# First projections fed from two weight streams, with their conversions ranked ahead of the normalisation

## The chip, the cores and the metric

The kernel runs on one core of one Trainium2 chip. The metric is device microseconds (us) for one execution, the median of several runs. Before the change it is 1677.1 us (three runs, 1676.74 to 1680.07).

## What is computed

One layer of a hybrid trunk on 512 tokens of width 1024, all in float32. Its first steps are what the change touches:

```
h  = rmsnorm(x, norm_mix)                  # x: 512 x 1024
u  = h @ w_in                              # 1024 x 15,616 columns; RWKV, HGRN2, Mamba-2 and gate columns
xw, xa, xg, dt                             # 64 + 64 + 160 + 32 "tail" columns of u
log_w = -exp(-softplus(-(w0 + tanh(xw) @ w_up)) - 0.5)
a     = sigmoid(a0 + xa @ a_up)
y_a, y_b, y_c = rwkv7(u), hgrn2(u), mamba2(u)
merged = gate0*(y_a @ wb0) + gate1*(y_b @ wb1) + gate2*(y_c @ wb2)
x = x + merged @ w_out;  h = rmsnorm(x, norm_ffn)
x = x + (silu(h @ wg) * (h @ wu)) @ w_ffn_out;  out = rmsnorm(x, norm_final)
```

## The kernel before

Every dense product is done in three TensorE passes: activations and weights are each split into a high part (rounded to fp32r) and a low part (the rest), and high times high, high times low and low times high are added in one PSUM bank. The normalised activations are kept transposed as `hh` and `hl`, [128 x 8 x 512].

Weights come in granules of 512 values per partition. `wcols` (L596) makes one: one or two DMAs into a raw tile, a copy on ScalarE (ACT) into the high tile, a subtraction on VectorE (DVE) into the low tile. A stream is a set of places: stream `w` has two raw places (`wr`) and four high and low ones (`wh`, `wl`), L1629; stream `rg` has two of each (`rgr`, `rgh`, `rgl`), L1406. A third raw tile of a stream can be loaded only when the first has been converted and subtracted.

`front` (L683) loads x in four tiles, normalises them and transposes them through PSUM into `hh` and `hl`, first for tokens 0 to 255, then for 256 to 511 (`norm_half`, L648). `tails` (L712) then makes the first projections: 128 columns into bank `d` (two granules) and 64 columns into bank `g` (one granule of 8 x 64, loaded by two DMAs of 8 x 32 columns), both by `dense_halves` (L663), which does each half of the tokens separately, and 128 columns into bank `rw` (two granules) by `dense_h`. From `d`, `g` and `rw` come the inputs of the RWKV decay and gate. `r_stage1` (L794) is the first step of a pair of RWKV heads and takes its weights from stream `rg`; the other mixers and the gates fill TensorE between the steps of the eight pairs.

What order each engine runs is not the order of the code. All operations are recorded with a rank `prio`, and `flush` (L302) lists them: at each step the engine that is free first takes, of its operations that are ready by the planner's own costs, the one with the lowest rank, and among equals the one recorded first. `front` is recorded at rank 0, `tails` and the first `r_stage1` at rank 1, HGRN2 at 2, Mamba-2 at 3, the gates at 4, the merge at 5, the tail of the layer at 6. A granule's DMAs, copy and subtraction take at most rank `WP` = 1. On the chip each engine runs its list strictly as written; SyncE (SP) issues all DMAs from one list.

Of the kernel before, what the change touches and what calls it, by code (L numbers as in the profile page):

```python
# [20 lines left out]
P = 128  # L21
# [5 lines left out]
OFF_TAIL = 3 * RW  # L27
# [4 lines left out]
OFF_DT = OFF_XBC + 3072  # L32
# [42 lines left out]
class Queue:  # L75


    def __init__(self, rec, name):
        self.rec, self.name = rec, name
# [330 lines left out]

class Kern:
    WP = 1

    def __init__(self, tc, ctx, A, consts, out):
        self.tc, self.nc, self.ctx, self.A, self.out = tc, Recorder(tc), ctx, A, out
# [180 lines left out]
    def wcols(self, W, r0, kk, pieces, st="w"):  # L596


        nc = self.nc
        pool, size, bufs, rsize, rbufs = self.wst[st]  # L600
        n = kk * sum(w for _, w in pieces)
        raw = self.t(pool, [P, rsize], st + "r", bufs=rbufs)
        wh = self.t(pool, [P, size], st + "h", dt=F32R, bufs=bufs)
        wl = self.t(pool, [P, size], st + "l", dt=F32R, bufs=bufs)
        v = lambda x: x[:, 0:n].rearrange("p (k c) -> p k c", k=kk)
        prio, nc.prio = nc.prio, min(nc.prio, self.WP)
        c = 0
        for c0, w in pieces:
            nc.sync.dma_start(out=v(raw)[:, :, c:c + w],
                              in_=W[r0:r0 + kk * P, c0:c0 + w].rearrange("(k p) c -> p k c", p=P))  # L610
            c += w
        nc.scalar.copy(out=wh[:, 0:n], in_=raw[:, 0:n])
        self.nlo += 1
        eng = nc.vector if self.lo_dve and self.nlo % self.lo_dve == 0 else nc.gpsimd
        eng.tensor_tensor(out=wl[:, 0:n], in0=raw[:, 0:n], in1=wh[:, 0:n].bitcast(F32), op=ALU.subtract)
        nc.prio = prio
        return v(wh), v(wl)
# [94 lines left out]
    def tails(self, rk):  # L712

        nc, A, cp = self.nc, self.A, self.mx
        W = A["w_in"][0]
        r = lambda tag: self.t(cp, [P, S], tag, dt=F32R)
        lain, sg0, sg1 = (self.t(rk, [P, S], g) for g in ("Ei", "kk", "k"))
        ps2, ps, ps3 = self.psg(), self.psd(), self.psr()
        self.dense_halves([(ps, W, [(OFF_TAIL, P)]), (ps2[0:64], W, [(OFF_TAIL + 256, 32), (OFF_DT, 32)])], lambda: "w")
        self.load_consts(rk)  # L720
        self.load_params0(rk)
        self.dense_h(ps3, [(OFF_TAIL + P, P)], "w")
        self.mix(lain, ps, self.pc("mu", 24), self.omu[:, 24:25])
        H = (slice(0, 64), slice(64, 128))
        nc.scalar.activation(lain[H[0]], lain[H[0]], AF.Tanh)

        self.lora = [r("xw"), r("xa")]
        for i, x in enumerate(self.lora):
            nc.scalar.copy(out=x[H[i]], in_=lain[H[i]])
            nc.vector.tensor_tensor(out=x[H[1 - i]], in0=lain[H[i]], in1=x[H[i]].bitcast(F32), op=ALU.subtract)  # L730
        self.mix(sg1[0:32], ps2[0:32], self.mu1[:, 0:1], self.mu1[:, 1:2])
        nc.scalar.activation(sg1[0:32], sg1[0:32], AF.Sigmoid)
        self.mix(sg0, ps3, self.pc("mu", 25), self.omu[:, 25:26])
        nc.scalar.activation(sg0, sg0, AF.Sigmoid)
        self.sg0 = (r("sg0h"), r("sg0l"))
        self.split(*self.sg0, sg0)

        self.sg1 = r("sg1")
        for b in (0, 32):
            nc.scalar.copy(out=self.sg1[b:b + 32], in_=sg1[0:32])  # L740
        nc.vector.tensor_tensor(out=self.sg1[64:96], in0=sg1[0:32], in1=self.sg1[0:32].bitcast(F32), op=ALU.subtract)

        self.dto = self.t(rk, [P, 4, P], "Ot")
        for c in range(NT):
            nc.vector.tensor_copy(out=self.dto[c * 32:c * 32 + 32, 0], in_=ps2[32:64, c * P:(c + 1) * P])
# [913 lines left out]
```

## Time and profile before

| | |
|---|---|
| median of three runs | 1677.1 us |
| the profiled execution | 1676.58 us, span 1674.8 us |
| TensorE (PE) busy | 1620.5 us, 97% |
| VectorE (DVE) busy | 1023.8 us, 61% |
| ScalarE (ACT) busy | 849.3 us, 51% |
| DMA | 192.08 MB, 115 GB/s over the span |
| chain that ended last | PE 71%, DVE 5%, ACT 4%, DMA 4% |

The span runs from the first to the last instruction of the profiled execution; 1.8 us of its time lie around it. A row of a timeline gives the start, the duration, the engine, the line, the operation and its tiles; the bracket says how long the engine had been idle before and what ended that. Matmuls of one run overlap in the records, so their cost is the distance between their starts.

### The profile page before, as it was taken

Reading aid. Unit: us, or ns where it says so; the run is one execution under the profiler, and the core shown is the slowest. Engines: PE = TensorE matmul, PEld = TensorE weight load, DVE = VectorE, ACT = ScalarE, POOL = GpSimd, SP = SyncE. Lnnn points to the kernel's source line nnn. Section 1 sums busy time; section 2 is a strip of 40 time slices with the busy share of each in tenths; the row PEclk is TensorE's granted clock in tenths of the full one; section 3 lists DMA queues with packets and bytes.
Section 4 is the critical chain, followed back from the end, with each engine's and each line's share of the span. In section 5 each row is a group of like instructions: output and inputs, shape, how many; then the busy total and the mean of one; then the engine's idle time right before and its main releaser. Section 6 shows DMA issues by size and latency. Waiting matters only on the chain.

```text
span 1674.8 us, 31996 instructions
## 1 busy us (share of the span) xinstructions
PE 1620.5 (97%) x12302; PEld 1317.1 (79%) x12302; DVE 1023.8 (61%) x2327; ACT 849.3 (51%) x1533; POOL 262.8 (16%) x285
## 2 busy tenths in 40 slices
PE   6999999999998999999999999999999999999998
PEld 5787787778777877787897787777888888888886
DVE  5787978878887879557558646344354433333233
ACT  6656655655565556567468745324334433333222
POOL 1123231322132222012033112011020000000000
PEclk9999999999999999999999999999999999999999
DMA  5333324333233334334434545877472333333232
GB/s 166 81 90 87 85 69 101 90 96 79 69 86 84 85 78 112 91 98 114 111 107 143 166 124 187 256 213 227 151 223 74 110 94 95 94 94 94 97 95 76
DMA packets 291320, 192.08 MB, mean 115 GB/s; under 512 B 59053, under 2 KB 255047, under 8 KB 291167
## 3 DMA queue, kind: packets, MB, share of 16 engines
q1 hardware_dynamic: 291167, 190.04, 39.8%
q8 instruction: 96, 1.57, 0.4%
q14 instruction: 57, 0.47, 0.1%
HBM read 164.22 MB, written 25.76 MB: 113 GB/s over the span
## 4 chain that ended last, share of the span: by engine, by line
PE 71%; DVE 5%; ACT 4%; DMA 4%; issue 2%; SPq 0%; POOL 0%; POOLq 0%; ACTq 0%; DVEq 0%
PE d L402 20%; PE rd L402 13%; PE g L402 9%; PE m L402 8%; PE rw L402 7%; PE rs L402 7%; PE ru L402 7%; ACT L399 1%; DMA ydram<-y 1%; DMA em<-ydram 1%; DVE cb L402 1%; DMA ab<-ydram 1%; DVE X L402 1%; DMA gwr<-in_w_in_dram 1%; DMA cb<-dcum 0%
## 5 line engine op out<-in xcount | busy, mean ns | idle before, releaser
L402 DVE TENSOR_TENSOR wl<-wr,wh 128x512 fp32r<-128x512 f32 x267 | 187.4, 703 | 260.7 <-ACT wh L402 256.9
L402 ACT CAST wh<-wr 128x512 fp32r<-128x512 f32 x267 | 164.8, 619 | 321.4 <-PE d L402 97.4
L402 ACT CAST rgh<-rgr 128x512 fp32r<-128x512 f32 x142 | 87.8, 618 | 192.7 <-PE rd L402 96.3
L402 DVE TENSOR_TENSOR rgl<-rgr,rgh 128x512 fp32r<-128x512 f32 x142 | 102.0, 719 | 107.0 <-ACT rgh L402 105.0
L402 PE MATMUL d<-hh,wh 128*128 128x512 f32 (+1 forms) x368 | 148.2, 403 | 4.7 <-ACT sg L402 2.5
L399 ACT ACT_TABLE_LOAD x115 | 147.5, 1283 | 2.0
L402 PE MATMUL d<-hh,wl 128*128 128x512 f32 (+1 forms) x368 | 145.8, 396 | 1.1 <-DVE wl L402 1.1
L402 PE MATMUL d<-hl,wh 128*128 128x512 f32 (+1 forms) x368 | 145.4, 395 | 0.0
L402 PE MATMUL rd<-hh,rgh 128*128 128x512 f32 (+1 forms) x324 | 130.1, 402 | 2.8 <-DVE k L402 1.6
L402 PE MATMUL rd<-hh,rgl 128*128 128x512 f32 (+1 forms) x324 | 128.2, 396 | 0.0
L402 PE MATMUL rd<-hl,rgh 128*128 128x512 f32 (+1 forms) x324 | 128.0, 395 | 0.0
L402 PEld LDWEIGHTS d<-hh,wh 128*128 128x128 f32 x368 | 70.1, 190 | 22.4 <-ACT sg L402 3.3
L402 PE MATMUL g<-hh,gwh 128*128 128x512 f32 x192 | 79.3, 413 | 7.8 <-ACT gwr L402 4.4
L402 PEld LDWEIGHTS d<-hh,wl 128*128 128x128 f32 x368 | 70.0, 190 | 16.2 <-DVE wl L402 1.4
L402 PEld LDWEIGHTS d<-hl,wh 128*128 128x128 f32 x368 | 69.9, 190 | 13.4 <-issue 1.0
L402 PE MATMUL g<-hh,gwl 128*128 128x512 f32 x192 | 78.4, 409 | 0.2
L402 PE MATMUL g<-hl,gwh 128*128 128x512 f32 x192 | 76.7, 400 | 0.0
L402 PE MATMUL d<-wh,hh 128*128 128x256 f32 x256 | 74.3, 290 | 2.0 <-DVE q L402 0.9
L402 PEld LDWEIGHTS rd<-hh,rgh 128*128 128x128 f32 x324 | 60.9, 188 | 19.3 <-DVE k L402 2.7
L402 PE MATMUL d<-wl,hh 128*128 128x256 f32 x256 | 73.2, 286 | 0.0
L402 PE MATMUL d<-wh,hl 128*128 128x256 f32 x256 | 72.6, 284 | 0.0
L402 PEld LDWEIGHTS rd<-hh,rgl 128*128 128x128 f32 x324 | 60.9, 188 | 14.2 <-issue 0.5
(1514 smaller groups left out, 4235.8 us busy)
## 6 DMA issues: line engine op xcount, KB each, us to landing
wr<-in_w_in_dram SPq DMA_DIRECT2D x108, 256.0 KB
rgr<-in_w_in_dram SPq DMA_DIRECT2D x88, 256.0 KB
wr<-in_w_branch_dram SPq DMA_DIRECT2D x59, 256.0 KB
wr<-in_w_ffn_in_dram SPq DMA_DIRECT2D x58, 256.0 KB
gwr<-in_w_in_dram SPq DMA_DIRECT2D x96, 128.0 KB
rgr<-in_w_ffn_in_dram SPq DMA_DIRECT2D x30, 256.0 KB
wr<-in_w_ffn_out_dram SPq DMA_DIRECT2D x30, 256.0 KB
gdram<-gwr SPq DMA_DIRECT2D x24, 256.0 KB
```

The costliest lines, as they stand in the source:

```text
L399: self.nc.scalar.preload_act_table_set(ops[-1 - j][7])
L402: getattr(getattr(self.nc, eng), method)(*[self.resolve(x) for x in args], **{k: self.resolve(x) for k, x in kw.items()})
```

## The change

The five granules of the first projections no longer all come from stream `w`: an iterator gives them `w`, `rg`, `w`, `rg`, `w`. So the first granule of `d` is `wr`, the second `rgr`, the 64-column granule of `g` is `wr`, the two of `rw` are `rgr` and `wr`. Then, for the three granules of `dense_halves` alone, copy and subtraction get rank -1 (`WC`), ahead of the normalisation's 0; their DMAs keep rank 1. For all later granules `WC` equals `WP` and nothing changes in rank.

```diff
 class Kern:
     WP = 1
+    WC = 1
...
             c += w
+        nc.prio = min(prio, self.WC)
         nc.scalar.copy(out=wh[:, 0:n], in_=raw[:, 0:n])
...
         lain, sg0, sg1 = (self.t(rk, [P, S], g) for g in ("Ei", "kk", "k"))
+
+        early = iter(("w", "rg", "w", "rg", "w")).__next__
+        self.WC = -1
         ps2, ps, ps3 = self.psg(), self.psd(), self.psr()
-        self.dense_halves([(ps, W, [(OFF_TAIL, P)]), (ps2[0:64], W, [(OFF_TAIL + 256, 32), (OFF_DT, 32)])], lambda: "w")
+        self.dense_halves([(ps, W, [(OFF_TAIL, P)]), (ps2[0:64], W, [(OFF_TAIL + 256, 32), (OFF_DT, 32)])], early)
+        self.WC = self.WP
         self.load_consts(rk)
         self.load_params0(rk)
-        self.dense_h(ps3, [(OFF_TAIL + P, P)], "w")
+        self.dense_h(ps3, [(OFF_TAIL + P, P)], early)
```

Because the list is made anew, the order of the whole mixer part moves. PE has 7369 rows of order before and 7426 after (equal instructions in sequence are one row; the instructions are as many). Leaving out the buffer numbers, the orders of PE read alike from row 5184 of before on, which is in the last gate matmuls; the merge, the output projection and the feed-forward part keep their order. ACT loads its tables 116 times before and 112 times after.

In the order before, this is SP's list in the stretch where the 64-column granule is loaded (`wr_232`, by its two DMAs 128x8x32) and then the first granule of `rw` (`wr_295`); `Bt` and `v` are parameters of later steps.

```order
L402 DMA wr_232<-in_w_in_dram 128x8x32
L402 DMA Bt_211<-in_rwkv_gn_b_dram 8x128
L402 DMA Bt_211<-in_hgrn_gn_w_dram 8x128
L402 DMA Bt_211<-in_hgrn_lb_logits_dram 8x128
L402 DMA Bt_211<-in_norm_ffn_dram 8x128
L402 DMA Bt_211<-in_ssm_conv_b_dram 24x128
L402 DMA Bt_211<-in_ssm_gn_w_dram 16x128
L402 DMA v_282<-in_ssm_conv_w_dram 24x512
L402 DMA wr_232<-in_w_in_dram 128x8x32
L402 DMA wr_295<-in_w_in_dram 128x4x128
```

SP's list after the change, from the first weight DMA; the 64-column granule is `wr_108`, those of `rw` are `rgr_159` and `wr_190`, and `E`, `mu`, `a` and `cst` are small parameters and constants.

```order
L402 DMA wr_101<-in_w_in_dram 128x4x128
L402 DMA rgr_103<-in_w_in_dram 128x4x128
L402 DMA wr_108<-in_w_in_dram 128x8x32
L402 DMA cst_110<-in_shape_constants_dram 128x384
...
L402 DMA E_118<-in_rwkv_r_k_dram 8x128
L402 DMA mu_49_150<-in_rwkv_mu_dram 32x1
L402 DMA rgr_159<-in_w_in_dram 128x4x128
L402 DMA a_166<-in_rwkv_w_up_dram 64x128 x2
L402 DMA a_166<-in_rwkv_a_up_dram 64x128 x2
L402 DMA wr_190<-in_w_in_dram 128x4x128
L402 DMA wr_108<-in_w_in_dram 128x8x32
L402 DMA rgr_200<-in_w_in_dram 128x4x128
```

The 64-column granule's first DMA stood in row 28 of SP and is now in row 9; its second stood in row 36 and is now in row 23, behind all four `a` DMAs and `wr_190`, before the `Bt` rows.

ACT's list before, from its last activations of `front` to the read of bank `d` (`Ei`); `rgh` and `gwh` are copies of granules for the first RWKV pair and the first gate.

```order
L402 ACTIVATE hh_168<-m_209,par_135 128x256
L402 CAST rgh_268<-rgr_179 128x512
L402 ACTIVATE hh_168<-rs_236,par_135 128x256
L402 CAST rgh_278<-rgr_183 128x512
L402 CAST gwh_285<-gwr_194 128x256
L402 CAST gwh_289<-gwr_201 128x256
L402 CAST wh_345<-wr_295 128x512
L402 CAST wh_353<-wr_232 128x512
L402 ACTIVATE Ei_362<-d_218,omu_298 128x512
```

ACT's list after, from the last of the four squares of `front`; each `hh` row is an activation of `front`.

```order
L402 ACTIVATE BKt_154,nss_106<-KAo_99 128x1024
L402 CAST wh_170<-wr_101 128x512
L402 CAST rgh_177<-rgr_103 128x512
L402 ACTIVATE hh_182<-m_126,par_136 128x256
...
L402 ACTIVATE hh_182<-rs_131,par_136 128x256
L402 CAST rgh_227<-rgr_159 128x512
L402 ACTIVATE hh_182<-ru_134,par_136 128x256
L402 ACTIVATE hh_182<-m_222,par_136 128x256
L402 CAST wh_250<-wr_190 128x512
L402 ACTIVATE hh_182<-rd_174,par_136 128x256
L402 CAST wh_264<-wr_108 128x512
L402 ACTIVATE hh_182<-m_222,par_136 128x256
```

All five copies now stand among or ahead of the sixteen activations that write `hh`; before, two stood among them and three behind.

PE's list before, at the end of bank `d`'s second half and the start of `rw` and `g`.

```order
L402 MATMUL d_218<-hh_168,wh_203 128x256
L402 MATMUL d_218<-hl_176,wh_203 128x256
L402 MATMUL d_218<-hh_168,wl_276 128x256
L402 MATMUL rw_359<-hh_168,wh_345 128x512
L402 MATMUL rw_359<-hl_176,wh_345 128x512
L402 MATMUL g_366<-hh_168,wh_353 64x256
L402 MATMUL g_366<-hl_176,wh_353 64x256
L402 MATMUL rw_359<-hh_168,wl_356 128x512
```

PE's list after: the end of `d`'s first half, then the borders to `d`'s second half and to `rw`.

```order
L402 MATMUL d_188<-hl_198,rgh_177 128x256
L402 MATMUL d_188<-hh_182,rgl_185 128x256
L402 MATMUL g_290<-hh_182,wh_264 64x256
L402 MATMUL g_290<-hl_198,wh_264 64x256
...
L402 MATMUL g_290<-hh_182,wl_278 64x256
L402 MATMUL d_188<-hh_182,wh_170 128x256
L402 MATMUL d_188<-hl_198,wh_170 128x256
...
L402 MATMUL g_290<-hh_182,wl_278 64x256
L402 MATMUL m_421<-ident_93,E_118 128x66
L402 MATMUL rw_423<-hh_182,rgh_227 128x512
```

Before, `d`'s 48 matmuls came in one piece and those of `g` and `rw` after them; now 24 of `g` stand between the two halves of `d`, 24 behind, and `rw` last.

## Rows read from the trace of the kernel before

**Rows 1.** Busy time by stretch: start:end, length, engines' busy us, PEclk, DMA share, GB/s.
```profile
23.50:26.67 3.17, 0.00 (x1) 0.00 (x1) 0.02 (x1) 0.67 (x2) 0.00 (x0) 1.00 0.85 205
26.67:39.54 12.87, 12.87 (x72) 11.52 (x73) 8.18 (x15) 8.94 (x14) 0.45 (x1) 0.87 0.48 132
39.54:100.00 60.46, 60.46 (x395) 48.39 (x394) 49.36 (x122) 42.54 (x74) 15.49 (x15) 1.00 0.31 80
100.00:1200.00 1100.00, 1066.27 (x9657) 864.77 (x9656) 765.52 (x1864) 623.51 (x1131) 227.76 (x238) 1.00 0.42 119
```

**Rows 2.** PE's timeline, from `d`'s waits to the first HGRN2 matmul.
```profile
19.21 0.39 PE L402 MATMUL d<-hh,wl 128*128 128x256 f32 x1 [0.69 <-DVE wl L402]
19.43 0.28 PE L402 MATMUL d<-hh,wh 128*128 128x256 f32 x1
...
23.21 0.28 PE L402 MATMUL d<-hh,wl 128*128 128x256 f32 x1
26.67 0.50 PE L402 MATMUL rw<-hh,wh 128*128 128x512 f32 x1 [3.17 <-ACT wh L402]
...
35.12 0.40 PE L402 MATMUL rw<-hh,wl 128*128 128x512 f32 x1
...
39.54 0.39 PE L402 MATMUL rs<-xw,lwh 128*128 128x512 f32 x1
...
40.53 0.29 PE L402 MATMUL m<-ident,Bt 82*128 82x82 f32 x1
...
41.34 0.50 PE L402 MATMUL d<-hh,wh 128*128 128x512 f32 x1
```

**Rows 3.** ACT's timeline: activations into `hh`, copies of weights, the long wait.
```profile
10.42 0.82 ACT L402 ACTIVATE hh<-m,par 128x256 fp32r<-128x256 f32 x2
...
12.56 1.17 ACT L402 CAST wh<-wr 128x512 fp32r<-128x512 f32 x2
...
26.00 1.14 ACT L402 CAST wh<-wr 128x512 fp32r<-128x512 f32 x2 [5.49 <-DMA wr<-in_w_in_dram]
```

**Rows 4.** SP's timeline: start and length of DMA issues.
```profile
10.25 0.27 SPq L402 DMA_DIRECT2D E<-in_rwkv_k_a_dram  x1
11.03 0.27 SPq L402 DMA_DIRECT2D E<-in_rwkv_r_k_dram  x1
11.52 0.32 SPq L402 DMA_DIRECT2D mu<-in_rwkv_mu_dram  x1
...
13.13 1.24 SPq L402 DMA_DIRECT2D a<-in_rwkv_a_up_dram  x2
...
19.07 0.38 SPq L402 DMA_DIRECT2D wr<-in_w_in_dram  x1
...
22.17 1.01 SPq L402 DMA_DIRECT2D wr<-in_w_in_dram  x2
```

**Rows 5.** What SP waited for from 7.9 to 12 us: total, times, longest.
```profile
SPq L402 <- DMA wr<-in_w_in_dram: 1.1, 2, 0.6
```

**Rows 6.** Busy time in half microseconds: 256 KB granules (17.0), then the 128 KB of 8x32 columns.
```profile
17.00:17.50 0.50, 0.00 (x0) 0.00 (x0) 0.50 (x2) 0.50 (x3) 0.00 (x0) 1.00 1.15 346
20.00:20.50 0.50, 0.50 (x7) 0.50 (x5) 0.44 (x3) 0.50 (x2) 0.00 (x0) 1.00 0.61 98
20.50:21.00 0.50, 0.50 (x7) 0.50 (x6) 0.50 (x1) 0.01 (x1) 0.00 (x0) 1.00 1.11 176
```

**Rows 7.** DVE's timeline: parts of `hl`, subtractions of weights.
```profile
10.91 0.87 DVE L402 SCALAR_TENSOR_TENSOR hl<-m,par,hh 128x256 fp32r<-128x256 f32 x2
...
13.93 0.68 DVE L402 TENSOR_TENSOR wl<-wr,wh 128x512 fp32r<-128x512 f32 x1
```

**Rows 8.** The page's group of table loads on ACT: busy us, mean ns, idle before.
```profile
L399 ACT ACT_TABLE_LOAD x115 | 147.5, 1283 | 2.0
```

**Rows 9.** A stop of PE among the mixers, in PE's timeline.
```profile
126.95 0.65 PE L402 MATMUL d<-hh,wh 128*128 128x512 f32 x1 [2.19 <-ACT sg L402]
```

**Rows 10.** Busy time in the five microseconds around that stop.
```profile
125.00:130.00 5.00, 3.05 (x8) 2.36 (x9) 3.31 (x10) 4.80 (x6) 0.59 (x1) 0.71 0.60 144
```

## The prediction made before the run

> **What bounds the kernel now.** I read the page's busy shares first: PE is busy for 97% of the span, so the time is PE's work plus PE's idle time plus what a lower clock costs, and since the change neither adds nor removes a matmul, only the last two can move. Then I read busy time by stretch, to find where PE is idle. From 39.54 to 100 us it is not idle at all; from 100 to 1200 us it is idle for 33.7 us of 1100, in many small pieces [rows 1]. The longest piece of the whole run after the first instructions lies at 23.50 to 26.67 us, in the stretch that the diff touches. PE's timeline says who ends it: PE stops 3.17 us for ACT's copy of a weight granule, after 0.69 us for a subtraction a little earlier [rows 2]. ACT's timeline says why the copy is late: ACT itself waits 5.49 us for the DMA [rows 3]. And SP's timeline says why the DMA is late: the 64-column granule (`wr_232`) goes out at 19.07 and, with its second half and the first granule of `rw`, at 22.17 [rows 4]; both raw places of stream `w` were in use until the first two granules were subtracted, and then SP stood behind its parameter rows. So the head of the kernel is bound by two raw places and a list of DMAs.
>
> There is a second cost of that stop. PE's clock is at its full 2.4 GHz while PE is stopped, and in the next stretch, 26.67 to 39.54, the mean granted clock is 0.87 [rows 1]: PE worked for a while at 1.2 GHz. The work there is 48 matmuls of `g` at 0.118 us (33 starts from 19.43 to 23.21 are that far apart) and 24 of `rw` at 0.233 us (19 starts from 35.12 to the next instruction at 39.54) [rows 2]: 5.7 + 5.6 = 11.3 us. It took 12.87, so the low clock cost about 1.6 us.
>
> **The change, part by part.** When is the 64-column granule usable now? Its raw place is free from the start, so its first half goes out early. SP's later waits date the early loads: the three issues at 10.25, 11.03 and 11.52 [rows 4] came when the two weight granules and the constants had landed (SP's waits there are for `wr`, twice [rows 5]). The first half of the new granule is now ahead of the constants in the same list, 128 KB in rows of 128 bytes. The same load took 0.61 + 1.11 shares of half a microsecond, 0.86 us of all DMA engines, where a 256 KB granule moves at 346 GB/s, 0.38 us for as many bytes [rows 6]. So `mu` moves from 11.52 to 12.4, `rgr_159` goes out at 12.75, four `a` issues follow at about 0.62 us each (two took 1.24 [rows 4]) until 15.8, then `wr_190`, then the granule's second half at 16.3. These two are the pair that went out at 22.17 before, in the other order, and were used at 26.00 [rows 3, 4]: 3.8 us. The granule is usable at 15.8 + 3.8 = 19.6 instead of 26.0.
>
> The Trainium skill speaks against that small-row load (DMA: Bandwidth & Descriptors, "Specifications": full rate needs at least 512 bytes; below, the engine reads, modifies and writes). The trace agrees: at the rate of the large granule each half would land 0.5 us earlier, and the sum below would be 1 us better; the measured 0.86 us is what I use.
>
> Copy and subtraction: ACT takes 0.6 us for the copy (two in 1.17 [rows 3]), DVE 0.7 for the subtraction [rows 7]. `g` can start at 20.3 and runs freely from 21.0.
>
> What is paid for it: two copies (1.17 us) now stand ahead of the first `hh` on ACT, and two subtractions (1.3 us) ahead of most of `hl` on DVE; two further copies that wait for DMAs stand among the `hh` rows, so what is behind them on ACT (the last `hh` rows, later `rgh` and `gwh` copies) waits too. DVE then needs nine parts of `hl` at 0.44 (two in 0.87 [rows 7]) after about 13.1, so the first half of `d` cannot end before 17.1; with `rgh_227` waiting for `rgr_159` until 16 to 17 it ends at 17.5 to 18.8. All that is hidden: PE waits for `g`'s granule until 20.3 anyway. Were the granule there at 17, this chain would decide, and the rank -1 would cost what it now hides, some 1.5 us. The second half's `hh` and `hl` rows (six parts, 2.6 us, after 21.0) are due only when `g`'s first 24 matmuls are done, and k by k after that.
>
> PE from there: 22 matmuls of `g` to 23.6, 24 of `d` to 26.4, 24 of `g` to 29.3, a transpose of 0.25, 24 of `rw` at 0.233 to 35.1. Before, `rw` ended at 39.54. Gain: 4.4 us. What is late next is the input of the decay product `rs`. From the end of `g` ACT has to read two banks, load a table (1.28 us [rows 8]), apply two functions and make two copies at about 0.6 us each, and DVE makes two subtractions: 29.3 + 1.3 + 6 x 0.6 + 1.4 = 35.6, or about 36.3 if the copy of an HGRN2 granule that stands ahead of it waits for its DMA. PE has 0.8 us of parameter transposes ahead of `rs` now (40.53 to 41.34 before [rows 2]), so it needs the input at 35.9. I take 0.4 us for this, bounds 0 and 1. Gain 4.0.
>
> The clock: PE stands idle from about 18 to 20.3 and briefly to 21.0, shorter than the 3.17 us that was followed by the low clock, longer than the 0.69 that was not. Bounds: nothing, or a stretch like that of before, 1.6 us. The Trainium skill (TensorE: Matmul & The Clock Gate, "HAM oscillation") has it that a long enough wait for a load throttles PE, so that the next work starts at half rate. If this stop is long enough by that rule, the gain is 2.4 and not 4.0; the trace shows it after one of its two stops at the head. I take the middle, 0.8. Gain 3.2.
>
> The mixers: the planner packs 100 to 1200 us anew. No matmul is added, PE is full from 39.54 to 100 before, so nothing there swallows a shift as long as ACT (42.5 of 60.5 us) and DVE (49.4) keep up [rows 1]. What can change is which stops occur among the mixers. One such stop: PE waits 2.19 us for ACT to read bank `d` [rows 9], because that read stands behind a copy and a table load; and in these 5 us PE is idle for 1.95 us and the clock is 0.71, 1.45 us more [rows 10]. 3.4 us for one stop, either way, and of 33.7 us of idle time there may be several more or fewer. The order gives no sign for one direction (four table loads less on ACT, some more changes of bank on PE), so I take nothing, and keep two such stops, 6.8 us, as both ends.
>
> Sum: 3.2 us off the profiled execution's 1676.58 gives 1673.4. That execution lies 0.5 us under the median of the three runs, so against the median of 1677.1 it is 3.7 us, 0.22%. Differences under 0.2%, 3.4 us, count as no change.
>
> **The rivals.** (1) Slower: the new packing of the mixers meets more stops of PE behind ACT's reads of the banks `d` and `g`, with the low clock behind them. Place: between 100 and 1200 us. Price 3.4 us each; one more cancels the gain, two make it 1680.2, three 1683.6. For it: each bank of these streams exists once, and the table loads stand in front of their reads. Against it: nothing in the change aims there. (2) The same packing meets one stop less and PE's clock holds at the head: 1676.6 - 4.0 - 3.4 = 1669.2. (3) The gain at the head is given back: the copies for the first RWKV pair, made ahead before, now come just in time (their stream carries two of the early granules), and PE stops for them between 36 and 100 us. For it: DVE is busy for 49.4 of 60.5 us there. Against: PE reaches the second of them only some 5 us after `rs`, long after its DMA. 1676.6. (4) The change doesn't do what it says, because the granule's second half, behind the `a` rows on SP, lands late after all. Since `d`'s second half now stands behind `g` on PE, each us of lateness costs one; from 24.7 instead of 20.3 on there is no gain, and if it came at 26.0 as before, the time would be 2 us worse than before, 1678.6.
>
> **How the numbers follow.** Forecast (1670 to 1676): 46%, of it 28 below the bound of 0.2% and 18 within. Rival 1: 16%, slower. Rival 2: 17%, faster. Rival 3: 16%, 14 within and 2 slower. Rival 4: 5%, 3 within and 2 slower. Together faster 45%, within 35%, slower 20%. The likeliest case's own range is 1670 to 1676; the range for 8 in 10 reaches to one stop less at one end and two more at the other, 1667 to 1681.
>
> **What would show it.** In the changed profile: SP issues the second 8x32 load near 16.3; ACT copies the 64-column granule near 19.6; PE's longest stop after its first instruction is about 2.5 us and ends near 20.3 at `g`; no 3 us stop near 24; `rw` ends near 35 (36.8 with the low clock); `rs` follows without a stop over 1 us; PE is full to 100 us. It is wrong if the copy of the 64-column granule begins after 23, if `rs` still starts near 39, or if PE's idle time between 100 and 1200 us differs from 33.7 by more than 4 us: then the packing decides, and not the head.

## The result, and the profile after

The changed kernel takes 1685.1 us, the median of five runs (1682.68 to 1690.36), against 1677.31 us before in the same session (five runs, 1676.74 to 1680.07): a ratio of 1.0051, 95% interval 1.0032 to 1.0069. It is slower, outside the predicted range. Its profiled execution took 1684.33 us, its span is 1682.3 us. Of 7.5 us more span PE is busy for 4.2 (1624.7 after 1620.5, with the same 12,302 matmuls) and idle for 3.3.

The head first. SP's timeline of the changed kernel, with the issue that answers to the last of [rows 4]:

```profile
15.82 1.06 SPq L402 DMA_DIRECT2D wr<-in_w_in_dram  x2
```

The row holds two issues: the second granule of `rw` at 15.82 and the 64-column granule's second half behind it, at 16.37 in the trace (predicted were 15.8 and 16.3). Their counterparts of before went out from 22.17 on. ACT's timeline, as [rows 3]:

```profile
19.99 0.61 ACT L402 CAST wh<-wr 128x512 fp32r<-128x512 f32 x1
...
27.23 0.62 ACT L402 CAST wh<-wr 128x512 fp32r<-128x512 f32 x1 [3.66 <-DMA wr<-in_w_in_dram]
29.85 0.62 ACT L402 CAST wh<-wr 128x512 fp32r<-128x512 f32 x1 [2.00 <-PE m L402]
30.37 0.62 ACT L402 CAST rgh<-rgr 128x512 fp32r<-128x512 f32 x1
31.98 0.62 ACT L402 CAST wh<-wr 128x512 fp32r<-128x512 f32 x1 [0.98 <-DMA wr<-in_w_in_dram]
32.50 0.68 ACT L402 ACTIVATE k<-g,mu 32x512 f32<-32x512 f32 x1
...
36.24 0.62 ACT L402 CAST xw<-Ei 64x512 fp32r<-64x512 f32 x1
```

The granule's copy begins at 19.99 (19.6 predicted). Four copies for later granules stand ahead of the reads of the banks (`k`, `Ei`), three of them behind the end of `g` on PE (29.6). The first of these three waits for PE, the last for its DMA until 31.98; the copy `xw` runs only from 36.24 to 36.86. PE's timeline, as [rows 2]:

```profile
20.65 0.33 PE L402 MATMUL g<-hh,wh 128*64 128x256 f32 x1 [1.97 <-ACT wh L402]
...
21.38 0.33 PE L402 MATMUL g<-hh,wl 128*64 128x256 f32 x1 [0.28 <-DVE wl L402]
...
35.07 0.39 PE L402 MATMUL rw<-hh,wl 128*128 128x512 f32 x1
...
37.72 0.47 PE L402 MATMUL rs<-xw,lwh 128*128 128x512 f32 x1 [1.60 <-DVE xw L402]
```

`g` starts at 20.65 (20.3 predicted), and `rw`'s last matmul gives way to the next row at 35.30 (35.1 predicted, 39.54 before). Up to there everything is where the prediction put it. Then PE stops 1.60 us for the input of `rs`, which DVE finishes with a subtraction behind ACT's copy.

Busy time by stretch shows the rest; the columns are those of [rows 1].

```profile
35.30:39.54 4.24, 2.64 (x12) 1.50 (x10) 3.05 (x7) 4.11 (x8) 0.00 (x0) 1.00 0.05 16
39.54:100.00 60.46, 56.90 (x323) 44.32 (x324) 47.94 (x125) 41.26 (x68) 12.65 (x13) 0.94 0.31 79
100.00:1200.00 1100.00, 1064.93 (x9684) 865.94 (x9684) 764.77 (x1857) 615.91 (x1129) 241.03 (x240) 0.99 0.43 117
```

From 39.54 to 100, where PE was never idle, it is now idle for 3.6 us at a clock of 0.94. From 100 to 1200 it is idle for 35.1 us, only 1.4 more than before, yet the clock reads 0.99 in place of 1.00. So the idle time in the mixers hardly changed, and the clock did. These are the five-microsecond windows of the changed kernel, after 40 us, with a granted clock under 0.8:

```profile
40.00:45.00 5.00, 5.00 (x16) 3.96 (x17) 3.92 (x16) 4.94 (x9) 0.00 (x0) 0.68 0.10 23
90.00:95.00 5.00, 4.88 (x14) 3.88 (x15) 3.90 (x18) 4.34 (x6) 1.65 (x3) 0.66 0.02 5
320.00:325.00 5.00, 5.00 (x17) 3.66 (x15) 4.16 (x14) 3.27 (x5) 1.16 (x1) 0.69 0.41 129
370.00:375.00 5.00, 3.87 (x14) 2.26 (x16) 3.53 (x8) 2.79 (x7) 0.00 (x0) 0.59 0.40 125
375.00:380.00 5.00, 5.00 (x122) 4.56 (x122) 1.81 (x5) 1.19 (x3) 0.00 (x0) 0.73 0.13 36
455.00:460.00 5.00, 3.37 (x70) 3.37 (x74) 1.86 (x4) 1.41 (x4) 0.00 (x0) 0.66 0.10 15
915.00:920.00 5.00, 4.12 (x20) 3.78 (x21) 3.76 (x7) 3.14 (x7) 0.25 (x1) 0.70 0.15 56
920.00:925.00 5.00, 5.00 (x21) 4.28 (x22) 2.96 (x7) 1.50 (x5) 1.17 (x2) 0.62 0.56 184
```

The sum of (1 - clock) x 5 us over all windows from 40 to 1660 us, called *lost clock* below, is 13.5 us. It is 3.45 in the kernel before: the window of [rows 10] and the next, and one more at 515. Two of the eight windows, with 3.3 of the 13.5 us, lie ahead of 100 us; between 100 and 1200 us lost clock is 10.2 us, 6.8 more than before. Lost clock is the most that the low clock can have cost, since matmuls that wait for something else lose nothing. Each stretch has a stop of PE ahead of it. PE's timeline of the changed kernel around one of them, a stop as in [rows 9]:

```profile
90.12 0.50 PE L402 MATMUL rd<-hh,rgh 128*128 128x512 f32 x1 [2.44 <-ACT a L402]
90.46 0.39 PE L402 MATMUL rd<-hl,rgh 128*128 128x512 f32 x1
90.69 0.40 PE L402 MATMUL rd<-hh,rgl 128*128 128x512 f32 x1
90.92 0.57 PE L402 MATMUL rd<-hh,rgh 128*128 128x512 f32 x1
91.29 0.63 PE L402 MATMUL rd<-hl,rgh 128*128 128x512 f32 x1
...
93.85 0.63 PE L402 MATMUL rd<-hl,rgh 128*128 128x512 f32 x1
94.28 0.46 PE L402 MATMUL rd<-hh,rgl 128*128 128x512 f32 x1
94.57 0.39 PE L402 MATMUL rd<-hh,rgh 128*128 128x512 f32 x1
```

After 2.44 us without work the first matmuls start 0.23 us apart, those from 91.29 to 94.28 0.43 apart, then again 0.23: about 3.3 us at 1.2 GHz, some 1.5 us lost. Why PE stopped is told by ACT's timeline of the same kernel:

```profile
86.34 1.15 ACT L402 ACTIVATE X<-X 128x512 f32<-128x512 f32 x2 [0.25 <-DVE X L402]
87.51 1.28 ACT L399 ACT_TABLE_LOAD   x1
88.80 0.69 ACT L402 ACTIVATE tmpA<-rs,par 128x512 f32<-128x512 f32 x1
89.39 0.68 ACT L402 ACTIVATE a<-rd,par 128x512 f32<-128x512 f32 x1
```

Two exponentials of another mixer and a table load stand ahead of `tmpA` and `a`, which reads the bank that PE wants to write.

### The profile page after: what moved, and what is told of

Its sections match the earlier page's. It is cut to its first block, busy times and chain, and to the rows that moved or that the text cites. A ratio compares the mean times of both kernels' runs of the same rounds, so it can differ in the third digit from the quotient of the medians.

```text
span 1682.3 us, 31975 instructions
## 1 busy us (share of the span) xinstructions
PE 1624.7 (97%) x12302; PEld 1321.0 (79%) x12302; DVE 1023.7 (61%) x2327; ACT 843.1 (50%) x1529; POOL 273.0 (16%) x285
## 4 chain that ended last, share of the span: by engine, by line
PE 77%; DMA 8%; DVE 6%; ACT 5%; issue 2%; SPq 1%; POOL 0%; POOLq 0%; ACTq 0%; DVEq 0%
PE d L402 21%; PE rd L402 16%; PE g L402 9%; PE rw L402 8%; PE rs L402 8%; PE ru L402 8%; PE m L402 7%; DMA wr<-in_w_in_dram 2%; ACT L399 1%; DVE X L402 1%; DMA gwr<-in_w_in_dram 1%; SPq L402 1%; DMA ab<-ydram 1%; DMA em<-ydram 1%; DVE wl L402 1%
## 5 line engine op out<-in xcount | busy, mean ns | idle before, releaser
L402 PEld LDWEIGHTS rd<-hh,rgh 128*128 128x128 f32 x324 | 61.5, 190 | 19.6 <-ACT a L402 3.8
```

Of the source, the lines that this page charges most:

```text
L402: getattr(getattr(self.nc, eng), method)(*[self.resolve(x) for x in args], **{k: self.resolve(x) for k, x in kw.items()})
```

## The experiments

Two theories at first: the new packing of the mixers costs the time (P), or the first RWKV pair does, since its stream now also carries early granules (S). The first four kernels take the change apart by its two edits, then by place. All experiments were timed beside the kernel before, but in other sessions than the change, so the ratios are what to compare; all differences are under 1%.

**The streams alone** (copy and subtraction keep their rank):

```diff
-        self.WC = -1
+        self.WC = self.WP
```

> One part alone: the five early granules alternate between the streams, but their copies keep rank 1. Theory P (the loss lies in the new packing of the mixers): the packing is made anew here too, in a third way, so the time is not tied to that of the change: anywhere from 1673 to 1690 us, with the difference to before explained by PE's stops and low clock between 100 and 1200 us. Theory S (the loss comes from the rg stream, which now carries two early granules, so that the first RWKV pair and with it the chain of eight pairs start late): as slow as the change, 1683 to 1687 us.

Measured: 1678.1 us, ratio 1.0012 (1.0000 to 1.0025). S misses; P's range is so wide that it says little here.

**The rank alone:**

```diff
-        early = iter(("w", "rg", "w", "rg", "w")).__next__
+        early = iter(("w", "w", "w", "w", "w")).__next__
```

> The other part alone: all five early granules stay in stream w, and three of them are copied and subtracted ahead of the normalisation. Theory P: a fourth packing, 1673 to 1690 us. Theory S: the rg stream is as before, so the time is that of before, 1677 us, give or take 2.

Measured: 1674.88 us, ratio 0.9997 (0.9984 to 1.0009). The time is that of before, which is S's forecast, but the premise of P did not hold: this is hardly a new packing, since PE has the same instruction at the same place as before in 12,200 of 12,302 matmuls. For the streams alone it is 4839. So the new packing comes with the second stream, and this kernel shows what the earlier conversions are worth without it: nothing that can be measured, though its PE is idle for 4.6 us less up to 39.5 us.

**The new head with the mixers of before**, and **the head of before with the new mixers**: the planner's list is replaced by a stored one, made of the two kernels' lists (the last line of the diff puts that in words).

```diff
-        while left > len(order):
-            ...
+        order = head of one list + what is left, in the other's order
```

> The kernel with the change, but its operations are issued in a stored order: up to the end of bank g's matmuls the order of the change, and from there on every engine takes what is left in the order of before. Theory P: PE's stops and clock among the mixers are those of before, the head keeps most of its 4 us, so 1672 to 1677 us and mean clock near 0.996. Theory S: the early granules still use the rg places, so it is as slow as the change, 1683 to 1687 us.

> The reverse: the kernel before, issued up to the end of bank rw's matmuls in the order of before, and from there on in the order that the change gave to the mixers. Theory P: 1684 to 1690 us with a mean clock near 0.990, like the change. Theory S: the head and the streams are those of before, so 1677 us, give or take 2.

Measured: 1679.02 us, ratio 1.0017 (1.0003 to 1.0031), and 1683.51 us, ratio 1.0050 (1.0032 to 1.0068). The head and the streams of before with the new order of the mixers have the whole loss (0.5 us under P's range); the new head and streams have little of it. S falls. P holds in this, but its 1672 to 1677 for the new head was missed. The stops of over 1 us that PE's timeline of that kernel has between 33 and 46 us:

```profile
36.83 0.47 PE L577 MATMUL rs<-xw,lwh 128*128 128x512 f32 x1 [1.48 <-DVE xw L577]
41.85 0.50 PE L577 MATMUL rd<-hh,rgh 128*128 128x512 f32 x1 [1.96 <-ACT a L577]
```

Both wait for ACT's chain behind the banks: first for `xw`, and 5 us later for `a`. They take most of the head's gain back.

**Three stops to be taken out of the change** by moving ACT's instructions in a stored list (its rows in short):

```diff
-CAST wh (29.85)   -CAST wh (31.98)   ... CAST xa
+CAST xa   +CAST wh   +CAST wh
-ACTIVATE X x2   ACTIVATE tmpA   ACTIVATE a
+ACTIVATE tmpA   ACTIVATE a   ACTIVATE X x2
-CAST wh (455.38)   COPY UV   COPY UV
+COPY UV   COPY UV   CAST wh
```

> The changed program with three local moves in ScalarE's order and nothing else moved: the two copies into `rwh` that stand at 29.85 and 31.98 us go behind the copy of `xa` (they hold the input of `rs` back, PE's stop of 1.60 us at 37.72); `tmpA` and `a` of the second pair (88.80 and 89.39) go ahead of the two exponentials of `X` and their table load (PE's stop of 2.44 us at 90.12); the copy of wh that waited 6.72 us for its DMA at 455.38 goes behind the copies of `UV` (PE's stops of 4.0 us in 450 to 455). Theory P1 (the loss is the sum of single stops of PE, each with its stretch of half clock behind it): the stops give back 1.6 + 2.4 + 4.0 and the low clock behind them 1.6 + 1.7 + 1.7, at most 13.0 us, of which something comes back at other stops: 1673 to 1679, mean granted clock near 0.996. Theory P2 (the packing as a whole sets the length, and a stop that is taken away comes back at the next wait): 1682 to 1687, clock 0.989 to 0.991.

Measured: 1684.28 us, ratio 1.0045 (1.0028 to 1.0062): P2's numbers. But P1 was not tested cleanly, since two of the three stops stayed (1.51 us at `rs`, 1.93 at `a`) and only the third went. Why the first stayed is in DVE's timeline of this kernel:

```profile
35.55 1.29 DVE L576 TENSOR_TENSOR wl<-wr,wh 128x512 fp32r<-128x512 f32 x2 [2.37 <-ACT wh L576]
36.87 0.69 DVE L576 TENSOR_TENSOR xw<-Ei,xw 64x512 fp32r<-64x512 f32 x1
```

ACT's copy of `xw` ended at 34.23, 2.6 us earlier than in the change. DVE's list was left as it was, though: it first takes the subtractions of the two copies that were moved back, and gets to `xw` at 36.87, when it did in the change. At the second stop one of the two exponentials and the table load still ran ahead of `tmpA` (ACT's rows from 87.88). Four windows of this kernel are worth reading all the same:

```profile
40.00:45.00 5.00, 5.00 (x22) 4.04 (x23) 3.91 (x16) 4.94 (x8) 0.00 (x0) 1.00 0.10 24
90.00:95.00 5.00, 3.86 (x10) 3.04 (x11) 1.94 (x9) 4.92 (x7) 0.00 (x0) 0.66 0.23 57
70.00:75.00 5.00, 5.00 (x32) 3.34 (x30) 2.86 (x7) 2.04 (x4) 1.28 (x1) 0.61 0.42 111
455.00:460.00 5.00, 4.35 (x150) 3.85 (x146) 2.28 (x6) 2.24 (x6) 0.00 (x0) 1.00 0.51 125
```

The stop of 1.51 us ahead of 40 us is followed by the full clock here, and by 0.68 in the change; at 455 the low clock went with its stop; at 70 there is a new one, behind a stop of 1.12 us. In these traces the low clock comes behind stops; whether it comes differs from one stop to the next. And it differs between runs of one program: the twelve runs of this kernel go from 1677.01 us at a mean clock of 0.992 to 1692.14 at 0.984, with a correlation of -0.96.

**The first layer's tails ahead of all else in the new head** (ACT's rows in short):

```diff
-ACT: CAST wh, CAST rgh, CAST wh, read g, read d, ... CAST xw, CAST xa
+ACT: read d, CAST xa, ... CAST xw, CAST wh, read g, CAST rgh, CAST wh
```

> The changed head with the operations of the first layer's tails in an order of their own (ScalarE reads `Ei`, `xa` and `xw` right behind the d matmuls, ahead of the copies for the later weights; the 64-column granule's second half and the next granule are asked for ahead of the four loads of `a`), and the order of the kernel before for everything behind. Theory P: the head's gain of 3 to 4 us stays, the mixers go as before: 1671 to 1675. Rival (the head's gain is lost again in the first mixer pair whatever the order, since that pair waits for DMA and not for the head): 1676 to 1680, with stops of PE between 36 and 60 us.

Measured: 1677.94 us, ratio 1.0010 (0.9996 to 1.0025). These are the rival's numbers and place, but not its reason: `rs` starts at 35.57 after a stop of 1.53 us, and at 42.06 PE has stopped 2.71 us for ACT's `a`, not for a DMA; the clock in 40:45 is 0.50.

**Two repackings that have nothing to do with the change.** The planner's costs decide the order; two of them are altered a little in the kernel before.

```diff
-                t += 1.28
+                t += 1.31
```

> The kernel before, with one number of the planner's costs changed (a table load counted as 1.31 in place of 1.28). The work, its pools and the streams are those of before; up to the first four hundred matmuls PE's order is the same, behind them PE has the same instruction at the same place in 2622 of 9526. It is a new packing that has nothing to do with the first projections. Theory P (any new packing of the mixers meets another number of PE's stops, and the time goes with that number): off 1677 by 2 us or more to either side, 1671 to 1686, with the granted clock lower where it is slower. Rival (a packing as such costs nothing, only the change's operations do): 1675.5 to 1678.5.

```diff
-                return {"vector": 0.13, "sync": 2.0, "tensor": -0.3}.get(e, 0.0)
+                return {"vector": 0.14, "sync": 2.0, "tensor": -0.3}.get(e, 0.0)
```

> The kernel before, with another number of the planner's costs changed (the latency from VectorE to VectorE counted as 0.14 in place of 0.13): a second new packing, in which PE has the same instruction at the same place in 2985 of 9526. Theory P: off 1677 by 2 us or more to either side, 1671 to 1686. Rival: 1675.5 to 1678.5.

Measured: 1685.59 us, ratio 1.0050 (1.0033 to 1.0068), and 1686.44 us, ratio 1.0057 (1.0036 to 1.0079). P's ranges hold but for 0.4 us at the second, and the clock is lower. That the time goes with the number of PE's stops does not hold: between 30 and 1200 us the first has 26 stops over 0.45 us, 30.3 us together, and the kernel of the streams alone 34, 33.0 us, and that one is 0.4% faster. A packing made without the change costs as much as the change.

**The same two alterations in the changed kernel:**

```diff
 (the changed kernel)
-"vector": 0.13        -t += 1.28
+"vector": 0.14        +t += 1.31
```

> The changed kernel with the same number of the planner's costs changed as in the second repacking of the kernel before (VectorE to VectorE 0.14 in place of 0.13): the whole change, another packing. Theory Q (the change costs nothing of itself, its packing does, and packings spread over 1673 to 1687 whatever the change): anywhere in 1672 to 1688, and of this and the other repacked change one at 1680 or less. Rival R (the change itself costs the 8 us): 1682 to 1690 for both.

> The changed kernel with a table load counted as 1.31 in place of 1.28 by the planner: the whole change in a third packing. Theory Q: anywhere in 1672 to 1688, and of this and the other repacked change one at 1680 or less. Rival R: 1682 to 1690 for both.

Measured: 1688.32 us, ratio 1.0072 (1.0050 to 1.0094), and 1680.71 us, ratio 1.0019 (1.0005 to 1.0034). Neither is at 1680 or less, so Q is missed by 0.7 us; R falls by the second, if narrowly: its median lies 1.3 us below R's range, single runs reach up to 1685.

**The stops filled.** Now the cause itself: no instruction of the kernel moves, but PE gets matmuls of zeros to do where it stopped.

```diff
+                if j in FILL:
+                    self.fill(j, *FILL[j])
                 eng, method, args, kw = ops[j][:4]
...
+            self.nc.tensor.matmul(o, self.zero[:, 0:o.shape[0]], hh[:, 0, 0:w], start=not name, stop=not name, ...)
```

> The changed kernel in its own order, with 33 of PE's stops between 30 and 1200 us (all over 0.45 us in its trace, 33.3 us together) filled: ahead of the matmul that waited stand 1 to 17 matmuls of a zero weight tile with `hh`, as many as last about as long as the stop did. They add zero to a sum that is open at that moment, or write a bank that is free; nothing of the kernel's own work moves. Theory C (what the packing costs is the half clock that follows the stops): the stops stay as long, the low clock behind them goes, 1674 to 1679 us, mean granted clock 0.995 or more. Rival D (the half clock does not come from the stops, or the length of the stops themselves is the loss): 1682 to 1688 us, clock 0.988 to 0.991.

> The kernel before in its own order with 23 of its stops between 30 and 1200 us (25.9 us together) filled in the same way. Its trace has two stretches of low clock there, about 3.4 us, and its runs spread from clock 0.991 to 0.998. Theory C: 1671 to 1675 us, clock 0.997 to 0.999, and less spread than before. Rival D: 1675 to 1679, the spread as before; if the fill lasts longer than the stops do in most executions, some us more.

Measured: the change 1673.32 us (1671.30 to 1675.26), ratio to before 0.9981 (0.9970 to 0.9993); the kernel before 1673.8 us, ratio 0.9979 (0.9967 to 0.9991). D falls. C holds, though the change is 0.7 us below its range. The filled change is 11.8 us under the change of the first session, 0.70% by the ratios, and both are faster than the kernel before. Filled, the two are equal: the 0.51% that the change cost is gone. In the filled change's timeline of PE the fill ends where `rs` begins:

```profile
35.69 1.66 PE L467 MATMUL rd<-hh,zero 128*128 128x512 f32 x6
37.19 0.39 PE L445 MATMUL rs<-xw,lwh 128*128 128x512 f32 x1
```

And its busy time by window, two of those that had the low clock in the change and the long stretch:

```profile
40.00:45.00 5.00, 5.00 (x23) 4.00 (x23) 3.18 (x11) 4.94 (x10) 0.19 (x1) 1.00 0.26 72
370.00:375.00 5.00, 4.95 (x133) 4.02 (x131) 4.19 (x10) 1.29 (x3) 1.44 (x2) 1.00 0.29 77
100.00:1200.00 1100.00, 1088.47 (x9821) 882.71 (x9820) 769.89 (x1855) 620.85 (x1140) 238.32 (x240) 1.00 0.43 119
```

From 20 to 1660 us no window is below full clock. The page's busy shares of the filled change:

```profile
PE 1642.0 (98%) x12420; PEld 1332.7 (80%) x12420; DVE 1026.2 (61%) x2327; ACT 842.2 (50%) x1529; POOL 270.5 (16%) x286
```

Its zero matmuls alone, over nearly the whole span (stretch, length, busy us of PE, PEld and POOL):

```profile
0.00:1670.00 1670.00, 34.29 (x118) 21.16 (x118) 0.20 (x1) 1.00 0.40 115
```

Records of zero matmuls and of the kernel's own overlap by 5.7 us. Counted by themselves, the kernel's own matmuls are busy for 1642.0 - 34.3 + 5.7 = 1613.4 us, 11.3 less than in the change; the 13.5 us of lost clock are the most that it could be. PE is without own work for 1669.5 - 1613.4 = 56.1 us, 1.5 less than the 57.6 of the change, and its stops over 0.45 us between 30 and 1200 us come to 32.9 us after 33.3. So the stops stayed and the clock's part went: 11.3 and 1.5 are the 12.8 us by which the spans differ.

**The slowest two packings filled, and the rank alone filled:** the same edit, with each kernel's own stops.

```diff
-FILL = {stops of the filled change}
+FILL = {34, 28 and 22 stops of these kernels}
```

> The second repacking of the kernel before (1686.4 us) with 34 of its stops (33.6 us of them) filled with zero matmuls as in the filled change. Theory C1 (the half clock behind the stops is all that a packing costs): 1672 to 1676 us, as the other filled kernels, clock 0.997 to 0.999. Theory C2 (this packing's stops are longer as well): the clock as high, but 1677 to 1682.

> The repacked change that was slowest of all (1688.3 us) with 28 of its stops (28.5 us) filled in the same way. Theory C1: 1672 to 1676 us, clock 0.997 to 0.999. Theory C2: the clock as high, but 1677 to 1682.

> The rank alone (all five granules from stream `w`, copy and subtraction at rank -1; 1674.9 us when it ran) with 22 of its stops (25.3 us of them) filled with zero matmuls as in the filled change. Its trace has 4.6 us less idle time of PE up to 39.5 us than the kernel before, and PE's order in the mixers is close to that of before. Theory G (a shorter head is a gain as long as the mixers' packing and the clock stay): 1669 to 1671.5 us, 2 to 4 us below the filled kernel before (1673.8). Theory H (the mixers wait for other engines and give the head's gain back): 1672.5 to 1675.

Measured: 1687.2 us, ratio 1.0054 (1.0040 to 1.0068); 1681.43 us, ratio 1.0026 (1.0014 to 1.0037); and 1675.04 us, ratio 0.9981 (0.9969 to 0.9994), on a chip on which the kernel before took 1678.32. For the two packings C2 holds, for one beyond its figure: the clock is up (0.997 in both), and the packing of the change gives back 7 us, that of before nothing. The page's busy shares of the latter:

```profile
PE 1645.8 (98%) x12425; PEld 1334.5 (79%) x12425; DVE 1025.1 (61%) x2327; ACT 852.5 (51%) x1534; POOL 268.2 (16%) x286
```

And its zero matmuls alone:

```profile
0.00:1670.00 1670.00, 35.18 (x123) 21.60 (x123) 0.20 (x1) 1.00 0.41 114
```

With 6.8 us of overlap, its own matmuls fall from 1626.1 to 1645.8 - 35.2 + 6.8 = 1617.4 us, 8.7 less (lost clock fell by 8.6), and the time without own work rises from 60.8 to 1685.2 - 1617.4 = 67.8, 7.0 more: most of what the clock gave, the waits for the other engines took. Little of that is zero matmuls that outlasted their stop, though the fill was sized by one execution. Behind 29 of the 34 fills the kernel's own matmul starts within 0.2 us of the last semaphore that it waits for, and behind the other five it is late by 2.0 us in all. This packing is also idle for longer than the kernel before without any fill, 60.8 us against 54.3, so not all that it costs was clock to begin with. The third answers G against H by its ratio, equal to that of the filled kernel before (0.9979): H, though the intervals leave room for a gain of 2 us.

| kernel | us | ratio to before | lost clock, us |
|---|---|---|---|
| before | 1677.31 | | 3.45 |
| rank alone | 1674.88 | 0.9997 | 3.4 |
| new head, mixers of before | 1679.02 | 1.0017 | 5.15 |
| tails first | 1677.94 | 1.0010 | 7.35 |
| streams alone | 1678.1 | 1.0012 | 7.5 |
| change, repacked (table) | 1680.71 | 1.0019 | 6.8 |
| head of before, new mixers | 1683.51 | 1.0050 | 17.05 |
| change, ACT moved | 1684.28 | 1.0045 | 15.45 |
| **change** | 1685.1 | 1.0051 | 13.5 |
| before, repacked (table) | 1685.59 | 1.0050 | 11.95 |
| before, repacked (latency) | 1686.44 | 1.0057 | 10.25 |
| change, repacked (latency) | 1688.32 | 1.0072 | 12.95 |
| change, filled | 1673.32 | 0.9981 | 0 |
| before, filled | 1673.8 | 0.9979 | 0 |
| rank alone, filled | 1675.04 | 0.9981 | 0 |
| change, repacked (latency), filled | 1681.43 | 1.0026 | 1.75 |
| before, repacked (latency), filled | 1687.2 | 1.0054 | 1.7 |

The times are of several sessions, and lost clock is that of the profiled execution. The kernels without fill fall in two: 3 to 7.5 us of it up to a ratio of 1.002, 10 to 17 above. In the six of the second kind PE is busy for 4.2 to 9.1 us more than before with the same matmuls, while its idle time differs by -2.0 to 6.5 us. The last row shows that a high clock alone does not make a packing fast.

## Why the prediction was wrong

**The head up to `rw`: right.** Stop, copy, starts and the end of `rw` came within about 0.5 us of what was worked out from SP's list; 4.2 us were gained there, 4.4 predicted. The low clock that the prediction priced at 0.8 us for the stop at `g` did not come. The head of before has one more stop, which the prediction passed over, 1.42 us ahead of a transpose at 18.27, and no low clock followed that one either.

**The input of `rs`: the mechanism right, the size wrong.** The sum allowed 0.4 us, at most 1. It was 1.6 us, since three copies for later granules, not one, stood between the end of `g` and the reads, the last of them held by its DMA until 31.98. And the stop was followed by a low clock that this term did not contain (the 0.68 of 40:45, 1.6 us). Of the 4.2 us about 1 was left. The kernels with better heads show that the next link, `a`, would have taken the rest: a head that ends earlier gains only as far as ACT's and DVE's chain behind it is earlier too, and that was not worked through beyond `xa`.

**The other rivals.** Rival 3's place was right, 3.6 us of idle time from 39.54 to 100, but PE waits there for ACT's `a` (2.4 us) and for a product that DVE makes (`SB`, 1.1), not for the pair's weights. Rival 4 did not come: the second half landed in time.

**The mixers: the step that failed.** "I take nothing" put 0 with ends of 6.8 us on the new packing. The span grew by 7.5 us although 4.2 were gained up to `rw`; with 3.2 for `rs`, some 8.5 us fall to the rest. Idle time rose by 3.6 us from 39.54 to 100 and by 1.4 behind it, lost clock by 1.7 and 6.8; that this comes to more than 8.5 was not resolved, beyond lost clock being an upper bound. It is what rival 1 described, stops behind ACT with the low clock behind them, but part of it lies ahead of 100 us, and the price was more clock than stop.

Two assumptions of that step were wrong. That either direction is alike: of the orders tried in which the mixers are packed anew (the change, the streams alone, the new mixers behind the old head, four repackings, and the one with ACT moved), none is faster than before and six are slower by 0.45% or more, three of these with the change's own order. The three kernels that keep the mixers' order of before (the rank alone and the two with a new head, with 12,200 and more of PE's 12,302 matmuls in their old place) are within 0.2%. And that the price is in the count of stops: idle time from 100 to 1200 us rose by 1.4 us, so the test announced for it (4 us) would have passed, while lost clock rose by 6.8 in the same stretch and by 10 over all. There are more stops over 0.45 us between 30 and 1200, 33 (33.3 us) after 23 (25.9 us), but the streams alone have 34 (33.0 us) and lose 0.12%: what differs is how many of them drew the low clock. The Trainium skill (TensorE: Matmul & The Clock Gate, "A second HAM failure mode: psum-queue depth-cycling") says that frequent short idling between groups of matmuls lets the clock swing; the traces agree, with 0.59 and 0.73 in 370 to 380 behind stops of 0.84, 0.47 and 1.28 us within 5 us.

**Shown, and not shown.** Shown: the order of the mixers carries the loss (old head, new mixers), the change is not needed for it (repackings of before), and in the change it is the clock behind the stops (the fill leaves them as long and takes 11.3 us of busy time off, and the filled change is as fast as the filled kernel before). For the other packings that is shown in part at most: fill gave one 0.46% and one next to nothing. Not settled: why one packing's stops draw the low clock more often, why most orders are worse than that of before, and why the waits of the slowest packing grow once its clock is up.

## What to carry to other kernels

When a change makes a planner list the work anew, its own gain and the new list are two changes: price the list by running it without the change (a cost altered in the third digit), and only then believe a few microseconds of either sign. In a kernel whose PE is 97% busy, read the granted clock by small windows beside idle time, because 33.7 and 35.1 us of idle time came here with 3.45 and 10.2 us of lost clock. When instructions of one engine are moved, the lists of the engines that follow it have to move too. And stops that can't be removed can be filled: some 100 matmuls of zeros were worth 0.2% to the kernel before and 0.7% to the change, though next to nothing to one other packing.

## What the runs showed of the hardware

A stop of the same length does not always cost the same: 1.60 us ahead of `rs` was followed by 0.68 in 40:45, 1.51 us at the same place in another order by 1.00, and these two windows of the kernel before, with 3.49 and 2.62 us of idle time, are at full clock:

```profile
645.00:655.00 10.00, 6.51 (x47) 4.58 (x34) 9.81 (x35) 7.08 (x9) 0.00 (x0) 1.00 0.56 151
900.00:905.00 5.00, 2.38 (x13) 1.74 (x12) 4.62 (x10) 4.96 (x7) 2.75 (x3) 1.00 0.41 132
```

Matmuls whose weights are all zero hold the clock up too: with 118 of them in the change's stops it stayed full for 1640 us; in two other packings, with 98 and 123, 1.75 and 1.7 us of lost clock were left. And with the low clock goes the spread between runs: 15 us over twelve runs of the change with ACT moved, 4 us over twelve of the filled change.
